# Forming the combined gate and up weight blocks on POOL instead of VectorE, in a two-layer decoder trunk

## The chip, the core and the metric

The kernel runs on one core of a Trainium2 chip. The metric is the device time of one execution in microseconds (us), the median of three runs. Five engines run side by side, each through its own queue, in order: PE (TensorE, matrix products), DVE (VectorE), ACT (ScalarE), POOL (GpSimd) and SP (SyncE, which here only issues DMAs). They wait for each other by semaphores, so an instruction that waits also holds back everything behind it in its queue.

## The reference

Two decoder layers on a stream of 1024 tokens by 1024 features. Layer 0 mixes with a convolution module, layer 1 with stick-breaking attention. Both layers end in the same feed-forward part, which is where the change lies:

```python
def conv_gated_ffn(x, w_up, w_gate, conv_w, conv_b, w_down):
    u = x @ w_up
    g = causal_dwconv(x @ w_gate, conv_w, conv_b)
    return (jax.nn.silu(g) * u) @ w_down
...
        ffn = conv_gated_ffn(x, ffn_w_up[i], ffn_w_gate[i], ffn_conv_w[i], ffn_conv_b[i], ffn_w_down[i])
        ple = jax.nn.sigmoid(x @ ple_w_gate[i]) * (p[i] @ ple_w_proj[i])
        x = layer_norm(DN_ALPHA * x + ffn + ple, ln_ffn_g[i], ln_ffn_b[i])
```

All inputs are float32; w_up and w_gate are 1024 by 2816, w_down is 2816 by 1024.

## The kernel before

Every float32 product is made of three products of rounded parts: a number is split into a high part (rounded, made by ACT) and a low part (the number less its high part). `mm3` (L136 to L139) issues high by high (L137), high by low (L138) and low by high (L139); for a weight as the stationary side, L137 and L138 need its high part and L139 its low part.

The feed-forward part (`ffn_phase`) first adds the sigmoid-gated term `ple` (L246 to L261, which uses POOL at L259 and DVE at L261), then forms sums and differences of blocks of x (L276 to L284), and then loops over the 2816 hidden columns, 256 at a time, in 11 steps (L389). In each step `gate` makes 256 columns of x @ w_gate, `down` (for the step before) multiplies 256 hidden columns with w_down and adds the result to the residual tiles (L383, DVE), and `up` makes 256 columns of x @ w_up. `gate` and `up` both call `fast`, which computes a 2 by 2 block product with seven block products instead of eight (Strassen's scheme in Winograd's form). Its left factors are blocks of the weight and sums of them, its right factors blocks of x and sums of them.

`fast_w` (L286) prepares the left factors of one `fast`. Two DMAs from SP (L290) bring the halves r0 (with blocks a11, a12) and r1 (a21, a22). Four additions, L294, each 128 partitions by 512 numbers, form s1 = a21 + a22, a21 = a11 - a21 in place, s2 = s1 - a11 and, after a12 has been split, a12 = a12 - s2 in place. Seven `split` calls make the high part on ACT (L299) and the low part on POOL (L300, shown by the profile as L86, the line of the helper `sub_l`). There are 2 layers x 11 steps x 2 = 44 calls of `fast_w`, so 176 additions at L294.

All weight tiles come from one pool `wp` of eight slots, shown as `w`: the raw halves, the sums and the split parts, and the raw, high and low tiles of w_down (`load_w`, L126 to L133). One `fast_w` takes ten such tiles, so a tile is written only when PE, POOL or ACT has finished with the one that had its slot.

The seven block products go to PSUM tiles; DVE adds them up (L322). In `gate`, ACT and DVE then apply the three convolution taps (L348, L353) and ACT the silu (L355). In `up`, DVE multiplies (L364) and splits (L367, shown as L86 `f<-f`). The PSUM tiles (`big0`, `big1` and `bank0` to `bank3`) are used in turns by two groups of four halves; `down` writes its halves in turn, and the fifth may begin only when L383 has read the first.

The order of instructions in each queue is set when the kernel is built, by a scheduler that places them by its own estimates of durations (`schedule_with_timeline_sim`); the code above gives only what depends on what.

Of the kernel before, what the change touches and what calls it, by code (L numbers as in the profile page):

```python
# [51 lines left out]
def trunk_kernel(ctx: ExitStack, tc, x, p, a_pw1_w, a_pw1_b, a_dw_w, a_dw_b, a_ln_g, a_ln_b, a_pw2_w, a_pw2_b,  # L52
                 b_wq, kv_wk, kv_wv, b_wo, ln_mix_g, ln_mix_b, ffn_w_up, ffn_w_gate, ffn_conv_w, ffn_conv_b,
                 ffn_w_down, ple_w_gate, ple_w_proj, ln_ffn_g, ln_ffn_b, out, stop=None):
    nc = tc.nc
# [29 lines left out]
    def sub_l(eng, l, full, h):  # L85
        eng.tensor_tensor(out=l, in0=full, in1=h.bitcast(F32), op=ALU.subtract)  # L86
# [11 lines left out]
    def wslot(dt=F32):  # L98
        return wp.tile([P, 1024], dt, name="w", align_bytes=A4)
# [23 lines left out]
    def w_slab(src, kts, cols):  # L123
        return src.rearrange("(k p) n -> p k n", p=P)[:, kts, cols]
# [111 lines left out]
    def ffn_phase(i, xT, res, pp, g, b, sb, finish):  # L236
# [49 lines left out]
        def fast_w(w, f):  # L286
            cs = slice(f * P, (f + 2) * P)
            r0, r1, s = (wslot().rearrange("p (k n) -> p k n", k=4) for _ in range(3))
            for kb, r in enumerate((r0, r1)):
                nc.sync.dma_start(out=r, in_=w_slab(w[i], slice(kb * 4, kb * 4 + 4), cs))  # L290
            n0, n1 = slice(0, P), slice(P, 2 * P)

            def add(out, a, c, op):
                nc.vector.tensor_tensor(out=out, in0=a, in1=c, op=op)  # L294

            def split(full):
                hl = wslot(F32R).rearrange("p (o k n) -> p o k n", o=2, k=4)
                h, l = hl[:, 0], hl[:, 1]
                nc.scalar.copy(out=h, in_=full)  # L299
                sub_l(nc.gpsimd, l, full, h)  # L300
                return h, l

            a11, a21, a12, a22, s1, s2 = (t[:, :, ns] for t in (r0, r1, s) for ns in (n0, n1))
            add(s1, a21, a22, ALU.add)
            add(a21, a11, a21, ALU.subtract)
            add(s2, s1, a11, ALU.subtract)
            ws = [split(t) for t in (a11, s2, s1, a21, a12)]
            add(a12, a12, s2, ALU.subtract)
            return ws + [split(a12), split(a22)]
# [583 lines left out]
```

## Time and profile before

| what | value |
|---|---|
| median of 3 runs | 2701.26 us (2700.6 to 2705.1) |
| the profiled execution, its own time | 2710.24 us |
| its span, first to last instruction | 2708.1 us |
| PE busy | 2530.3 us (93%) |
| DVE busy | 1797.4 us (66%) |
| POOL busy | 1219.6 us (45%) |
| ACT busy | 1045.1 us (39%) |
| feed-forward loop of layer 0 | about 532 to 1190 us of the span |
| feed-forward loop of layer 1 | about 1990 to 2680 us |

The profile is of one execution. Its own time is 0.33% above the median. "Busy" is the time in which an engine works on an instruction. Matmuls overlap on PE, so PE can be busy without a gap and still be slower than it could be; the distance from one start to the next tells its pace.

### The profile page before, as it was taken

How to read it: one execution, taken by the hardware profiler on the slowest of the kernel's cores; microseconds unless marked ns; L12 is line 12 of the kernel's file. 1: busy time of each engine (PE TensorE's matmuls, PEld its weight loads, DVE VectorE, ACT ScalarE, POOL GpSimd, SP SyncE). 2: the span in 40 equal slices, each digit the busy share in tenths (PEclk: the TensorE clock that was granted, in tenths of full speed). 3: DMA queues.
4: the chain of work that ended last, by engine and by line, in shares of the span. 5: the costliest groups of instructions: out<-in, count | busy, mean ns of one | idle time of the engine just before them, and what ended most of it. 6: DMA issues, size and time to landing. Idle time of an engine off the chain costs nothing.

```text
span 2708.1 us, 34235 instructions
## 1 busy us (share of the span) xinstructions
PE 2530.3 (93%) x13300; PEld 2151.5 (79%) x13300; DVE 1797.4 (66%) x2785; ACT 1045.1 (39%) x1621; POOL 1219.6 (45%) x825
## 2 busy tenths in 40 slices
PE   8996898999999999999999999789899999999995
PEld 6884888987878787878888887589798787787874
DVE  4999769465565655675667677777845555655558
ACT  4556532333223332314555566632333232323231
POOL 3998236534333443413443433544744343333354
PEclk9998999999999999999999999899899999999998
DMA  4114421211111111123111101322111121111121
GB/s 151 47 47 148 163 71 63 86 47 50 47 60 47 55 55 55 40 80 108 46 43 36 55 25 47 129 84 87 63 63 62 48 63 47 47 47 47 47 78 62
DMA packets 149085, 179.12 MB, mean 66 GB/s; under 512 B 6508, under 2 KB 125756, under 8 KB 148924
## 3 DMA queue, kind: packets, MB, share of 16 engines
q1 hardware_dynamic: 144316, 168.56, 19.6%
q10 hardware_dynamic: 4608, 8.39, 0.8%
q8 instruction: 104, 1.70, 0.3%
q14 instruction: 57, 0.47, 0.1%
HBM read 151.76 MB, written 20.97 MB: 64 GB/s over the span
## 4 chain that ended last, share of the span: by engine, by line
PE 68%; DVE 18%; POOL 5%; DMA 3%; issue 3%; ACT 3%; SPq 0%; POOLq 0%; ACTq 0%; DVEq 0%
PE bank L137 13%; PE bank L138 13%; PE bank L139 13%; PE big L137 8%; PE big L139 7%; PE big L138 7%; POOL w L86 3%; PE big L739 2%; POOL pb L491 2%; DVE bank L502 2%; DVE bank L509 2%; DMA w<-in_ffn_w_up 2%; DVE pt L282 2%; PE bank L773 1%; PE more L779 1%
## 5 line engine op out<-in xcount | busy, mean ns | idle before, releaser
L86 POOL TENSOR_TENSOR w<-w 128x512 fp32r<-128x512 f32 (+1 forms) x444 | 757.7, 1720 | 1081.5 <-ACT w L299 697.0
L137 PE MATMUL bank<-w,xT 128*128 128x256 f32 x1280 | 369.7, 291 | 37.7 <-ACT sg L258 23.7
L299 ACT CAST w<-w 128x512 fp32r<-128x512 f32 x308 | 180.1, 619 | 540.2 <-PE bank L139 142.1
L138 PE MATMUL bank<-w,xT 128*128 128x256 f32 x1280 | 368.8, 290 | 2.1 <-POOL w L86 2.1
L139 PE MATMUL bank<-w,xT 128*128 128x256 f32 x1280 | 367.7, 290 | 0.7 <-DVE xT L86 0.6
L137 PEld LDWEIGHTS bank<-w,xT 128*128 128x128 f32 x1280 | 250.8, 197 | 41.0 <-ACT sg L258 25.1
L760 POOL TENSOR_TENSOR res<-res,rr 128x639 f32<-128x639 f32 (+3 forms) x96 | 152.6, 1590 | 259.7 <-DVE rr L758 237.9
L758 DVE TENSOR_TENSOR_SCAN rr<-rr,ctile 128x127 f32<-128x127 f32 (+7 forms) x128 | 195.7, 1550 | 102.5 <-ACT rr L756 102.1
L138 PEld LDWEIGHTS bank<-w,xT 128*128 128x128 f32 x1280 | 251.5, 197 | 3.4 <-POOL w L86 3.0
L139 PEld LDWEIGHTS bank<-w,xT 128*128 128x128 f32 x1280 | 250.2, 196 | 1.7 <-DVE xT L86 1.3
L132 ACT CAST w<-w 128x1024 fp32r<-128x1024 f32 x136 | 142.9, 1051 | 227.5 <-PE bank L138 60.5
L137 PE MATMUL big<-xT,w 128*128 128x512 f32 x544 | 212.3, 390 | 0.4 <-DVE xT L86 0.4
L138 PE MATMUL big<-xT,w 128*128 128x512 f32 x544 | 211.9, 389 | 0.0
L139 PE MATMUL big<-xT,w 128*128 128x512 f32 x544 | 211.9, 389 | 0.0
L294 DVE TENSOR_TENSOR w<-w 128x512 f32<-128x512 f32 x176 | 130.1, 759 | 106.1 <-DMA w<-in_ffn_w_up 52.1
L137 PE MATMUL bank<-xT,w 128*128 128x512 f32 x496 | 200.0, 403 | 0.3 <-DVE m L86 0.2
L138 PE MATMUL bank<-xT,w 128*128 128x512 f32 x496 | 198.2, 400 | 0.0
L139 PE MATMUL bank<-xT,w 128*128 128x512 f32 x496 | 197.8, 399 | 0.0
L383 DVE TENSOR_TENSOR m<-m,bank 128x512 f32<-128x512 f32 x192 | 128.8, 682 | 82.2 <-PE bank L139 82.1
L137 PE MATMUL bank<-w,f 128*128 128x512 f32 x448 | 170.3, 395 | 7.8 <-ACT f L366 4.3
L138 PE MATMUL bank<-w,f 128*128 128x512 f32 x448 | 176.1, 393 | 0.0
L139 PE MATMUL bank<-w,f 128*128 128x512 f32 x448 | 173.8, 391 | 0.0
(162 smaller groups left out, 5941.3 us busy)
## 6 DMA issues: line engine op xcount, KB each, us to landing
w<-in_ffn_w_gate SPq DMA_DIRECT2D x44, 512.0 KB
w<-in_ffn_w_up SPq DMA_DIRECT2D x44, 512.0 KB
w<-in_ffn_w_down SPq DMA_DIRECT2D x44, 512.0 KB
w<-in_a_pw_w SPq DMA_DIRECT2D x32, 512.0 KB
pp<-o ACTq DMA_DIRECT2D x32, 256.0 KB
w<-in_ple_w_gate SPq DMA_DIRECT2D x16, 512.0 KB
w<-pp SPq DMA_DIRECT2D x16, 512.0 KB
w<-in_b_wo SPq DMA_DIRECT2D x16, 512.0 KB
```

The costliest lines, as they stand in the source:

```text
L86: eng.tensor_tensor(out=l, in0=full, in1=h.bitcast(F32), op=ALU.subtract)
L132: nc.scalar.copy(out=h[:, 0:n], in_=raw)
L137: nc.tensor.matmul(out=o, lhsT=sh, rhs=mh, start=first, stop=False)
L138: nc.tensor.matmul(out=o, lhsT=sh, rhs=ml, start=False, stop=False)
L139: nc.tensor.matmul(out=o, lhsT=sl, rhs=mh, start=False, stop=last)
L282: nc.vector.tensor_tensor(out=f, in0=a, in1=c, op=ALU.subtract)
L294: nc.vector.tensor_tensor(out=out, in0=a, in1=c, op=op)
L299: nc.scalar.copy(out=h, in_=full)
L383: nc.vector.tensor_tensor(out=rv, in0=rv, in1=ps, op=ALU.add)
L491: nc.gpsimd.tensor_tensor(out=pb, in0=pb, in1=pr, op=ALU.add)
L758: nc.vector.tensor_tensor_scan(out=rv[:, i, 1:n][:, ::-1], data0=rv[:, i, 1:n][:, ::-1], data1=zero.broadcast_to([P, n - 1]), initial=1.0, ...
L760: nc.gpsimd.tensor_tensor(out=av[:, :, 0:n - 1], in0=av[:, :, 0:n - 1], in1=rv[:, :, 1:n], op=ALU.mult)
```

## The change

The additions at L294 are issued to POOL instead of DVE. The operation, its operands and its place in the code are the same.

```diff
             def add(out, a, c, op):
-                nc.vector.tensor_tensor(out=out, in0=a, in1=c, op=op)
+                nc.gpsimd.tensor_tensor(out=out, in0=a, in1=c, op=op)
```

The second `add` in `fast` (L322) is another function and stays on DVE. Since the scheduler places all instructions anew, orders and slots shift on every engine.

On DVE, at the end of the second step's `gate` in layer 0 (products in bank0 to bank3) and the start of `down` (halves in big0 and big1): bank tiles are gate products, f_5651 and f_5659 the gate's two output tiles, m_2587 a residual tile, w_5791 and w_5792 the raw halves for the next `up`, w_5793 its sums. Before:

```order
L322 TENSOR_TENSOR bank0_82<-bank0_82,pt_5557 128x512
L294 TENSOR_TENSOR w_5793<-w_5791,w_5792 128x4x128
L353 SCALAR_TENSOR_TENSOR f_5659<-bank3_85,ctile_86,f_5659 128x511
L322 TENSOR_TENSOR bank1_83<-bank1_83,pt_5584 128x512
L294 TENSOR_TENSOR w_5791<-w_5791 128x4x128
L294 TENSOR_TENSOR w_5793<-w_5793,w_5791 128x4x128
L353 SCALAR_TENSOR_TENSOR f_5659<-bank3_85,ctile_86,f_5659 128x510
L353 SCALAR_TENSOR_TENSOR f_5651<-bank0_82,ctile_86,f_5651 128x512
L353 SCALAR_TENSOR_TENSOR f_5651<-bank1_83,ctile_86,f_5651 128x511
L322 TENSOR_TENSOR bank2_84<-bank2_84,pt_5584 128x512
L383 TENSOR_TENSOR m_2587<-m_2587,big0_81 128x512
```

The same place now:

```order
L322 TENSOR_TENSOR bank0_82<-bank0_82,pt_5557 128x512
L353 SCALAR_TENSOR_TENSOR f_5659<-bank3_85,ctile_86,f_5659 128x511
L322 TENSOR_TENSOR bank1_83<-bank1_83,pt_5584 128x512
L353 SCALAR_TENSOR_TENSOR f_5659<-bank3_85,ctile_86,f_5659 128x510
L353 SCALAR_TENSOR_TENSOR f_5651<-bank0_82,ctile_86,f_5651 128x512
L353 SCALAR_TENSOR_TENSOR f_5651<-bank1_83,ctile_86,f_5651 128x511
L322 TENSOR_TENSOR bank2_84<-bank2_84,pt_5584 128x512
L353 SCALAR_TENSOR_TENSOR f_5651<-bank0_82,ctile_86,f_5651 128x512
L353 SCALAR_TENSOR_TENSOR f_5651<-bank1_83,ctile_86,f_5651 128x510
L383 TENSOR_TENSOR m_2587<-m_2587,big0_81 128x512
```

The three additions that stood between the last gate work and the first L383 are gone from DVE's queue.

On POOL, from the end of one `up` (w_5411 to w_5418) through the next `gate` (raw halves w_5527 and w_5528, sums w_5529; low parts w_5535 to w_5554). Before:

```order
L86 TENSOR_TENSOR w_5411<-w_5392,w_5411 128x512
L86 TENSOR_TENSOR w_5415<-w_5392,w_5415 128x512
L86 TENSOR_TENSOR w_5418<-w_5392,w_5418 128x512
L86 TENSOR_TENSOR w_5535<-w_5527,w_5535 128x512
L86 TENSOR_TENSOR w_5538<-w_5529,w_5538 128x512
L86 TENSOR_TENSOR w_5541<-w_5529,w_5541 128x512
L86 TENSOR_TENSOR w_5544<-w_5527,w_5544 128x512
L86 TENSOR_TENSOR w_5547<-w_5528,w_5547 128x512
```

Now:

```order
L86 TENSOR_TENSOR w_5411<-w_5392,w_5411 128x512
L294 TENSOR_TENSOR w_5392<-w_5392,w_5393 128x4x128
L86 TENSOR_TENSOR w_5415<-w_5392,w_5415 128x512
L86 TENSOR_TENSOR w_5418<-w_5392,w_5418 128x512
L294 TENSOR_TENSOR w_5529<-w_5527,w_5528 128x4x128
L86 TENSOR_TENSOR w_5535<-w_5527,w_5535 128x512
L294 TENSOR_TENSOR w_5527<-w_5527 128x4x128
L294 TENSOR_TENSOR w_5529<-w_5529,w_5527 128x4x128
L86 TENSOR_TENSOR w_5538<-w_5529,w_5538 128x512
L86 TENSOR_TENSOR w_5541<-w_5529,w_5541 128x512
L86 TENSOR_TENSOR w_5544<-w_5527,w_5544 128x512
L86 TENSOR_TENSOR w_5547<-w_5528,w_5547 128x512
```

The additions stand in POOL's queue in front of the low parts that need them, and the first addition of a `gate` or `up` stands there until both raw halves have landed.

On PE, in that `gate`, at the turn from its first block product (bank0) to the second. Before:

```order
L137 MATMUL bank1_83<-tT_4773,w_5538 128x512
L138 MATMUL bank1_83<-tT_4774,w_5538 128x512
L139 MATMUL bank1_83<-tT_4773,w_5538 128x512
L137 MATMUL bank1_83<-tT_4773,w_5538 128x512
L138 MATMUL bank1_83<-tT_4774,w_5538 128x512
L139 MATMUL bank1_83<-tT_4773,w_5538 128x512
L137 MATMUL bank1_83<-tT_4773,w_5538 128x512
```

Now:

```order
L137 MATMUL bank1_83<-tT_4773,w_5538 128x512
L138 MATMUL bank1_83<-tT_4774,w_5538 128x512
L137 MATMUL bank2_84<-tT_4771,w_5541 128x512
L138 MATMUL bank2_84<-tT_4772,w_5541 128x512
L137 MATMUL bank3_85<-tT_4775,w_5544 128x512
L138 MATMUL bank3_85<-tT_4776,w_5544 128x512
L139 MATMUL bank1_83<-tT_4773,w_5538 128x512
```

PE now takes the first two matmuls of three products, which need high parts only, before the first matmul that needs a low part (L139).

## Rows read from the trace of the kernel before

**Rows 1.** The page: span and busy time of each engine.

```profile
span 2708.1 us, 34235 instructions
PE 2530.3 (93%) x13300; PEld 2151.5 (79%) x13300; DVE 1797.4 (66%) x2785; ACT 1045.1 (39%) x1621; POOL 1219.6 (45%) x825
```

**Rows 2.** Window of layer 0's loop: length, busy time (count) by engine, granted clock, DMA share, GB/s.

```profile
680.00:800.00 120.00, 116.46 (x503) 94.91 (x503) 70.55 (x99) 36.91 (x52) 46.63 (x31) 0.99 0.15 44
```

**Rows 3.** Waits of PE, whole span: waiting and awaited instruction, us, times, longest.

```profile
PE big L137 <- DVE m L383: 24.9, 16, 3.0
```

**Rows 4.** Timeline of PE at the first long wait: start, length, instruction, idle before.

```profile
651.74 0.39 PE L138 MATMUL big<-w,f 128*128 128x512 f32 x1
651.97 0.39 PE L139 MATMUL big<-w,f 128*128 128x512 f32 x1
655.21 0.69 PE L137 MATMUL big<-w,f 128*128 128x512 f32 x1 [2.86 <-DVE m L383]
...
658.97 0.39 PE L137 MATMUL bank<-xT,w 128*128 128x512 f32 x1
```

**Rows 5.** Timeline of DVE there.

```profile
644.23 0.70 DVE L322 TENSOR_TENSOR bank<-bank,pt 128x512 f32<-128x512 f32 x1 [1.12 <-PE bank L139]
647.94 1.59 DVE L294 TENSOR_TENSOR w<-w 128x512 f32<-128x512 f32 x1 [3.01 <-DMA w<-in_ffn_w_up]
...
650.71 1.28 DVE L294 TENSOR_TENSOR w<-w 128x512 f32<-128x512 f32 x2
...
654.49 0.67 DVE L383 TENSOR_TENSOR m<-m,big 128x512 f32<-128x512 f32 x1
```

**Rows 6.** Windows of 20 us: without a wait, with long waits, with a short one.

```profile
620.00:640.00 20.00, 20.00 (x90) 16.56 (x89) 12.76 (x17) 8.34 (x13) 14.06 (x10) 1.00 0.21 67
...
648.00:668.00 20.00, 17.14 (x69) 13.74 (x68) 13.15 (x19) 6.03 (x8) 4.14 (x4) 0.91 0.00 1
898.00:918.00 20.00, 18.42 (x82) 14.93 (x81) 12.21 (x19) 7.08 (x11) 5.57 (x4) 1.00 0.03 11
2360.00:2380.00 20.00, 17.14 (x76) 13.87 (x75) 13.27 (x20) 6.54 (x9) 4.99 (x5) 1.00 0.00 1
684.00:704.00 20.00, 19.61 (x87) 15.92 (x86) 10.75 (x15) 7.80 (x11) 9.87 (x7) 1.00 0.16 53
```

**Rows 7.** Groups by line and shape: busy us, mean ns, then idle before and releasers.

```profile
L294 DVE TENSOR_TENSOR w<-w 128x512 f32<-128x512 f32 x176 | 130.1, 759 | 106.1 <-DMA w<-in_ffn_w_up 52.1 <-POOL w L86 50.6 <-DMA w<-in_ffn_w_gate 2.7
L86 POOL TENSOR_TENSOR w<-w 128x512 fp32r<-128x512 f32 x308 | 405.5, 1336 | 707.5 <-ACT w L299 697.0 <-DVE big L322 8.6 <-DVE f L353 1.9
L86 POOL TENSOR_TENSOR w<-w 128x1024 fp32r<-128x1024 f32 x136 | 352.3, 2590 | 374.0 <-ACT w L132 324.0 <-PE bank L139 19.5 <-DVE norm L179 5.9
L280 POOL TENSOR_TENSOR pt<-xT 128x512 f32<-128x512 f32 x32 | 50.9, 1613 | 10.9 <-DVE xT L86 10.2 <-DVE tT L86 0.6
L86 DVE TENSOR_TENSOR f<-f 128x1024 fp32r<-128x1024 f32 x44 | 71.4, 1640 | 3.5 <-ACT f L366 3.5
```

**Rows 8.** Timelines of POOL and ACT, from the end of `up` to the next `up`.

```profile
614.31 3.79 POOL L86 TENSOR_TENSOR w<-w 128x512 fp32r<-128x512 f32 x3 [18.04 <-ACT w L299]
...
626.50 5.05 POOL L86 TENSOR_TENSOR w<-w 128x512 fp32r<-128x512 f32 x4 [3.15 <-ACT w L299]
...
636.88 6.70 POOL L86 TENSOR_TENSOR w<-w 128x1024 fp32r<-128x1024 f32 x2 [1.33 <-ACT w L132]
...
625.80 1.66 ACT L299 CAST w<-w 128x512 fp32r<-128x512 f32 x3 [5.27 <-DVE w L294]
```

**Rows 9.** Timeline of PE: the `up`'s third product, and the `gate`'s first.

```profile
616.68 0.50 PE L137 MATMUL big<-tT,w 128*128 128x512 f32 x1 [0.22 <-ACT pt L326]
...
627.71 0.39 PE L137 MATMUL bank<-xT,w 128*128 128x512 f32 x1
```

**Rows 10.** The chain that ended last, at that place: start, us, what.

```profile
643.61 4.24 DMA w<-in_ffn_w_up
```

**Rows 11.** Window in attention's last part, columns as in Rows 2.

```profile
1680.00:1740.00 60.00, 44.14 (x228) 33.30 (x226) 47.23 (x60) 38.81 (x67) 21.99 (x15) 0.89 0.24 80
```

## The prediction

> **What bounds the kernel now.** I read the page first: PE is busy for 2530.3 of 2708.1 us, DVE for 66% and POOL for 45% [rows 1]. The loop that the change touches is tighter still. In 120 us of it, about two steps, PE is busy for 116.46 us, DVE for 70.55 and POOL for 46.63 [rows 2]. So no saving of DVE time counts by itself. Only a stretch in which PE stands still can be won, and only one in which it comes to stand still can be lost.
>
> The view of PE's waits says where it stands. Over the whole span the longest entry is PE waiting for DVE's L383, the addition that frees a PSUM half for `down`: 24.9 us in 16 waits, the longest 3.0 [rows 3]. All 16 lie in the two feed-forward loops, eight per layer; in each layer four are long (2.9 us, one in each layer less or without the after-effect told below) and four short (0.4 us).
>
> The timelines of the first long wait say why L383 was late. PE has finished four halves of `down` at 651.97 and starts the fifth at 655.21, released by L383 [rows 4]. DVE had begun nothing between 644.9 and 647.94: it stood for 3.01 us at an L294, whose weight half was still on its way from memory; that transfer is also on the chain that ended last, with 4.24 us [rows 5, 10]. From there to L383, at 654.49, it did three L294, four L353 and two L322. So PE waited for an addition that nobody needed yet, because it stood at the head of DVE's queue.
>
> What one such wait costs is more than its 2.86 us. From 651.97 to 655.21 are 3.24 us where the pace is 0.23, so 3.01 are lost; the nine starts from 655.21 to 658.97 take 3.76 us where they would take 2.07, so 1.69 more are lost at a lower clock [rows 4]. The granted clock over those 20 us is 0.91 of the 2.4 GHz level; the engine had been idle just before it fell. Together 4.70 us. The windows agree: 20 us without a wait hold 90 matmuls, those with this wait 69, and 21 matmuls at 20/90 = 0.222 us are 4.7 us [rows 6]. Six of the eight long waits have this window of 69. One (898 us) was shorter and has 82, so 1.8 us; one (2360 us) kept its clock at 1.00 and has 76, so 3.1 us [rows 6]. Sum: 6 x 4.7 + 1.8 + 3.1 = 33.1 us. A short wait has 87, so 0.7 us, and eight of them 5.4 us [rows 6].
>
> **The change, part by part.** *Taken from DVE:* 176 L294, 130.1 us busy, and the 106.1 us for which DVE stood before them, 54.8 of it for transfers and 50.6 for POOL [rows 7]. DVE is no bound, so this saves only what PE waited for. I work out when the first L383 comes without them, in the frame of rows 4 to 10 and at PE's pace of 0.227. The gate's first product starts at 627.71 [rows 9], and eight products of twelve matmuls, one of them the last of `up`, end at 649.5. DVE's last L322 waits for that, two L353 follow (0.66 each), and L383 can begin at about 651.6, when the first half of `down` is also ready. The new order on PE puts a product of the next `up` between the second half and the third, and there the halves of `down` go round two big tiles, so the half that L383 frees is wanted at 649.5 + 24 x 0.227 = 654.9. L383 then has 2.6 us to spare. The code and the order of DVE's queue are the same at the other long waits, so all 33.1 us go. For the eight short ones (behind L364 and the split of `up`, not behind L294) I take no change; they bound the gain at 33.1 + 5.4 = 38.5.
>
> *Added to POOL:* 176 additions of 128x512. The trace has none of L294 there. The nearest rows are the low parts of the same tiles, 1.336 us on average, and POOL's additions at L280 beside a busy DVE, 1.613 [rows 7]; three low parts in 3.79 us give 1.26 at the least [rows 8]. So 222 to 284 us; I take 1.35, the row with the same tiles, which makes 238. POOL's share in the loop goes from 46.63 to about 68 of 120 us (four `fast_w`, 16 additions). It stays under PE.
>
> The two engines slow each other when DVE has two inputs in SBUF: two low parts of 128x1024 took 6.70 us while DVE split a hidden tile, against 2.59 on average for one [rows 7, 8]. The Trainium skill (SBUF — State Buffer, Who interferes with whom) says the same as a rule: a DVE instruction with two SBUF inputs contends with a GpSimd instruction that reads SBUF, and the one that comes second waits. By that rule an addition on POOL could wait at most for the DVE splits, 44 of 1640 ns, 72 us in all if each hit one; the sum by the rows keeps 1.35.
>
> *Weights later.* POOL now works 4 x 1.35 = 5.4 us longer per `fast_w`, in series with the low parts. Whether PE feels it is read off one passage, from the end of an `up` to the next `up`, in the new orders of the queues and with each tile's slot as the new program gives it:
> - `up`'s three low parts end at 618.1 [rows 8]; addition to 619.45; high part on ACT, 0.70 from its start to the next low part (625.80 to 626.50) [rows 8]; two low parts to 622.8.
> - The second raw half for `gate` takes the slot that the `up`'s third product leaves at 616.68 + 12 x 0.227 = 619.4 [rows 9], lands 4.24 later at 623.65 [rows 10]. Addition to 625.0, low part of a11 to 626.3, two additions to 629.0, ACT 0.70, low part of s2 to 631.0. PE wants it after 24 + 6 matmuls from 627.71, at 634.5. Spare: 3.5 us.
> - Four more low parts and the last addition to 637.6; the last two low parts end at 639.5, where the last product starts at 646.8.
> - `down`'s two low parts, at the slow 3.35 each, end at 646.2, wanted at 649.5. Spare: 3.3.
> - The next `up`: its first raw half starts to load when the first of these is done (642.9), its second when PE has finished the gate's fifth product (644.0), landing at 648.3. Addition, low part of a11 to 650.9, wanted at 652.7. Spare: 1.8. Low part of s2 at 655.6, wanted at 658.6.
>
> So nothing is late, by 1.8 us at the tightest place. Behind a POOL addition that waits for a transfer stand only low parts of the same weights, except before the first step of each layer, where some L259 stand behind three additions and a low part (5.3 us). PE writes four tiles ahead there, so I take 0; uncovered it would be 5.3 per layer.
>
> *Moved elsewhere.* The scheduler also rearranged the last part of attention. The one window of it that has room has PE busy for 44.14 of 60 us [rows 11]. I take 0, and a quarter of the idle 15.9, 4 us, to either side.
>
> **Sum.** -33.1 for the long waits, 0 for the short ones, 0 for the weights. The profiled execution would go from 2710.2 to 2677. It stands 9 us above the median of 2701.3, so the median goes to 2668. I call a difference within 0.2%, about 5 us, no change, since three runs before spread over 4.5 us.
>
> **The rivals.**
> *Part of the gain goes into a new wait.* The 1.8 us at the next `up` are used up when a transfer takes 6 us in place of 4.24, or when POOL is held by DVE's split at that moment. There are four such passages a layer. A weight 2 us late at all eight costs 16, so 2684; the case covers 2678 to 2696. For it speaks that the scheduler itself lets PE take high parts first, as if low parts came late; against it, the spare times above.
>
> *L383 stays late.* If DVE's four L353 and two L322 (654.49 - 647.94 less 2.87 of L294, so 3.7 us of work) were what held L383, nothing is won: 2701, and 2696 to 2706 with attention's uncertainty. Against it, DVE's 3.01 us of standing and 2.9 us of L294 lie in the same 10 us [rows 5], and their sum, 5.9, is more than the wait.
>
> *POOL becomes the queue that holds PE.* The place is the low part of s2 in each `gate` and the one of a11 in each `up`: about 20 passages. Up to the spare time it costs nothing. Beyond, each us costs 20 us, so it eats up the 33.1 when the low parts come 1.7 us after PE wants them. That needs them 3.5 us (a11) to 5.2 us (s2) later than I worked out, for s2 1 us more on each of five POOL instructions. At 2.5 us late it costs 50, so 2718. The Trainium skill (GPSIMD Engine Reference, 4.1 Engine selection) advises against what the change does: elementwise work belongs on VectorE, since GpSimd takes about twice as long with two inputs. The trace agrees on the ratio, 1.34 us here against 0.64 for an undisturbed L294 [rows 5, 7]. It decides only if that length lies on PE's path, which the spare times deny.
>
> **How the numbers follow.** All long waits go, 2658 to 2678: 0.60. Part: 0.17. No change: 0.10. POOL holds PE, above 2706: 0.13. The likeliest gives 2668. The range begins at 2658, where the short waits and attention also gain (33.1 + 5.4 + 4, rounded), and reaches to 2702, through the second case and over half of the third: about 0.83. Faster by over 0.2% is 0.60 + 0.17, the same 0.10, slower 0.13.
>
> **What the changed profile would show.** Right: in PE's waits the entry for L383 falls from 24.9 to about 3 us, with no wait of over 1 us and the windows of 69 matmuls near 90; L294 on POOL at 1.3 to 1.6 us; POOL near 68 of 120 us in the loop. The step on DVE is wrong if L383 still releases PE after 2 us or more. The step on weights is wrong if PE waits at L139 for POOL's low parts, or at L137 for ACT's high parts. The prediction fails most simply if the transfers for `up` and `gate` land later than 4.24 us after their slot is free, since POOL now stands for them with every low part behind it.

## The result and the profile after

The changed kernel takes 2669.02 us, median of 4 runs (2666.01 to 2669.68), beside 2701.47 us for the kernel before (2700.6 to 2705.1, 4 runs): a ratio of 0.9867, 95% interval 0.9849 to 0.9884. The forecast was 2668.0, faster. In a later repeat the change measured 2666.57 and the kernel before 2695.9, ratio 0.9898 [0.9883, 0.9913].

The page of the changed kernel, its span and the busy time of each engine, which answers to [rows 1]:

```profile
span 2667.9 us, 34126 instructions
PE 2515.0 (94%) x13300; PEld 2144.1 (80%) x13300; DVE 1665.9 (62%) x2609; ACT 1040.3 (39%) x1621; POOL 1435.4 (54%) x1001
```

DVE lost 131.5 us and 176 instructions; POOL gained 215.8 us and the same 176. Two windows of layer 0's loop, the long one that answers to [rows 2] and 20 us around the first long wait of before, which answers to [rows 6]; columns as there:

```profile
680.00:800.00 120.00, 119.33 (x526) 98.28 (x526) 59.96 (x88) 36.19 (x52) 67.06 (x48) 1.00 0.17 53
646.00:666.00 20.00, 20.00 (x90) 16.54 (x90) 11.32 (x18) 7.44 (x11) 11.12 (x9) 1.00 0.09 26
```

In the same 120 us PE now starts 526 matmuls for 503, and the 20 us that held 69 hold 90, at a granted clock of 1.00. The waits of PE over the whole span, of which four entries matter here ([rows 3] is the one of before):

```profile
PE big L137 <- ACT pt L326: 6.3, 10, 0.7
...
PE bank L137 <- DVE m L383: 3.2, 3, 1.6
...
PE bank L139 <- POOL w L86: 1.3, 1, 1.3
PE bank L138 <- POOL w L86: 1.3, 3, 0.6
```

The entry of 24.9 us in 16 waits for L383 is gone, the short ones too; the 3.2 us left are three waits after the last loop, which the kernel before has as well. Something came in: ten waits for ACT's copy L326, 2.2 us in all before, are now 6.3. One wait in the loops is for a low part from POOL, 1.3 us.

DVE and PE of the changed kernel at the place of [rows 4, 5]: first DVE, then the starts on PE that matter.

```profile
649.95 0.69 DVE L322 TENSOR_TENSOR bank<-bank,pt 128x512 f32<-128x512 f32 x1
650.54 1.40 DVE L353 SCALAR_TENSOR_TENSOR f<-bank,ctile,f 128x512 f32<-128x512 f32 x2
651.86 0.68 DVE L383 TENSOR_TENSOR m<-m,big 128x512 f32<-128x512 f32 x1
```

```profile
649.44 0.39 PE L137 MATMUL big<-w,f 128*128 128x512 f32 x1
...
652.16 0.39 PE L137 MATMUL bank<-xT,w 128*128 128x512 f32 x1
...
654.88 0.39 PE L137 MATMUL big<-w,f 128*128 128x512 f32 x1
```

L383 starts at 651.86 and is done by 652.5. PE does two halves of `down`, a product of the next `up`, and comes back to `down` at 654.88: 2.3 us to spare.

Two things moved here at once. L383 starts 2.42 us after the first matmul of `down` (649.44), where it started 5.02 us after it before (649.47 to 654.49). And PE wants the half later by one product: before, that product of `up` came behind the half that waited,

```profile
657.84 0.63 PE L137 MATMUL bank<-xT,w 128*128 128x512 f32 x1
```

and now it comes ahead of it, at 652.16. How much either does by itself is taken up with the second and the third experiment.

What the additions cost on POOL, in the groups by line and shape that answer to [rows 7], and POOL's timeline through the tight passage, which answers to [rows 8]:

```profile
L294 POOL TENSOR_TENSOR w<-w 128x512 f32<-128x512 f32 x176 | 228.2, 1308 | 115.2 <-DMA w<-in_ffn_w_up 58.7 <-DMA w<-in_ffn_w_gate 49.6 <-issue 1.7
L86 POOL TENSOR_TENSOR w<-w 128x512 fp32r<-128x512 f32 x308 | 406.9, 1339 | 370.3 <-ACT w L299 370.2
L86 DVE TENSOR_TENSOR f<-f 128x1024 fp32r<-128x1024 f32 x44 | 61.4, 1402 | 18.9 <-ACT f L366 18.9
```

```profile
623.56 1.29 POOL L294 TENSOR_TENSOR w<-w 128x512 f32<-128x512 f32 x1 [0.92 <-DMA w<-in_ffn_w_gate]
...
629.33 5.06 POOL L86 TENSOR_TENSOR w<-w 128x512 fp32r<-128x512 f32 x4 [0.73 <-ACT w L299]
...
637.35 7.59 POOL L86 TENSOR_TENSOR w<-w 128x512 fp32r<-128x512 f32 x4 [0.73 <-ACT w L299]
648.64 1.30 POOL L294 TENSOR_TENSOR w<-w 128x512 f32<-128x512 f32 x1 [3.71 <-DMA w<-in_ffn_w_up]
649.89 1.30 POOL L86 TENSOR_TENSOR w<-w 128x512 fp32r<-128x512 f32 x1
```

The standing went with the additions: POOL now sits idle for 3.71 us at the head of its queue, where DVE sat for 3.01. But behind it stand only low parts of the weights that are on their way.

Where the time came from, by a marker: L348, which runs from the first `gate` of a layer's loop to the last. Layer 0 of the kernel before, then of the changed one (shortest, median and longest in ns, first and last start in us):

```profile
L348 ACT ACTIVATE f<-big,ctile x24: 760/774/780, 549.7 to 1099.1; 128x512 f32<-128x512 f32 x24
L348 ACT ACTIVATE f<-bank,ctile x20: 769/779/783, 645.0 to 1151.5; 128x512 f32<-128x512 f32 x20
```

```profile
L348 ACT ACTIVATE f<-big,ctile x24: 758/772/782, 550.4 to 1081.5; 128x512 f32<-128x512 f32 x24
L348 ACT ACTIVATE f<-bank,ctile x20: 762/778/782, 644.9 to 1135.1; 128x512 f32<-128x512 f32 x20
```

From 549.7 to 1151.5 are 601.8 us, from 550.4 to 1135.1 are 584.7: 17.1 less. Layer 1, by the same rows, goes from 603.3 to 587.4: 15.9 less. So 33.0 us of the 40.2 by which the two profiled spans differ lie in the loops. Another 7.7 lie between the last L348 of a layer and its last L383 (68.4 to 64.6 and 82.9 to 79.0); all the rest together is under 1 us.

A correction to the texts ahead: they speak of four halves of `down` before the long wait and of the fifth as the one that waits. A half takes six matmuls here (two hidden blocks by three), so the twelve from 649.5 to 651.97 are two halves, and the third waits. It writes the second 512 columns of a tile of 1024 of which L383 reads the first 512. The times in the prediction are those of the rows and do not change; what it means is the subject of the fourth experiment.

### The profile page after: what moved, and what is told of

The parts are those of the page before. It is cut to its first block, busy times and chain, and to the rows that moved or that the text cites. A ratio compares the mean times of both kernels' runs of the same rounds, so it can differ in the third digit from the quotient of the medians.

```text
span 2667.9 us, 34126 instructions
## 1 busy us (share of the span) xinstructions
PE 2515.0 (94%) x13300; PEld 2144.1 (80%) x13300; DVE 1665.9 (62%) x2609; ACT 1040.3 (39%) x1621; POOL 1435.4 (54%) x1001
## 4 chain that ended last, share of the span: by engine, by line
PE 76%; DVE 15%; POOL 3%; issue 3%; ACT 2%; DMA 1%; SPq 0%; POOLq 0%; DVEq 0%; ACTq 0%
PE bank L137 15%; PE bank L138 15%; PE bank L139 15%; PE big L137 8%; PE big L138 8%; PE big L139 8%; PE big L739 2%; DVE bank L502 2%; DVE bank L509 2%; DVE pt L282 2%; POOL pb L491 1%; PE bank L773 1%; PE more L779 1%; PE more L778 1%; DVE tT L86 1%
## 5 line engine op out<-in xcount | busy, mean ns | idle before, releaser
L86 POOL TENSOR_TENSOR w<-w 128x512 fp32r<-128x512 f32 (+1 forms) x444 | 744.0, 1689 | 733.6 <-ACT w L299 370.2
L137 PE MATMUL bank<-w,xT 128*128 128x256 f32 x1280 | 370.2, 292 | 32.1 <-ACT sg L258 23.6
L139 PE MATMUL bank<-w,xT 128*128 128x256 f32 x1280 | 367.6, 290 | 1.6 <-DVE xT L86 1.5
L294 POOL TENSOR_TENSOR w<-w 128x512 f32<-128x512 f32 x176 | 228.2, 1308 | 115.2 <-DMA w<-in_ffn_w_up 58.7
L137 PEld LDWEIGHTS bank<-w,xT 128*128 128x128 f32 x1280 | 250.8, 197 | 35.5 <-ACT sg L258 25.0
L139 PEld LDWEIGHTS bank<-w,xT 128*128 128x128 f32 x1280 | 250.1, 196 | 2.3 <-DVE xT L86 2.0
L137 PE MATMUL big<-xT,w 128*128 128x512 f32 x544 | 213.6, 393 | 0.6 <-DVE xT L86 0.6
L139 PE MATMUL big<-xT,w 128*128 128x512 f32 x544 | 212.8, 391 | 0.0
L137 PE MATMUL bank<-xT,w 128*128 128x512 f32 x496 | 197.5, 398 | 0.3 <-DVE m L86 0.2
L139 PE MATMUL bank<-xT,w 128*128 128x512 f32 x496 | 195.9, 395 | 1.3 <-POOL w L86 1.3
L138 PE MATMUL bank<-xT,w 128*128 128x512 f32 x496 | 195.9, 395 | 0.0
L383 DVE TENSOR_TENSOR m<-m,bank 128x512 f32<-128x512 f32 x192 | 128.4, 685 | 85.7 <-PE bank L139 85.6
L138 PE MATMUL bank<-w,f 128*128 128x512 f32 x448 | 174.4, 389 | 0.0
L139 PE MATMUL bank<-w,f 128*128 128x512 f32 x448 | 173.2, 389 | 0.0
L137 PE MATMUL bank<-w,f 128*128 128x512 f32 x448 | 166.1, 391 | 4.6 <-DVE m L383 3.2
```

Of the source, the lines that this page charges most:

```text
L137: nc.tensor.matmul(out=o, lhsT=sh, rhs=mh, start=first, stop=False)
L138: nc.tensor.matmul(out=o, lhsT=sh, rhs=ml, start=False, stop=False)
L139: nc.tensor.matmul(out=o, lhsT=sl, rhs=mh, start=False, stop=last)
L294: nc.gpsimd.tensor_tensor(out=out, in0=a, in1=c, op=op)
L383: nc.vector.tensor_tensor(out=rv, in0=rv, in1=ps, op=ALU.add)
```

## The experiments

My theory: PE lost time only where it waited for L383, and L383 was late because the additions of the next `up`, with the wait for their transfer, stood ahead of it on DVE. The main rival: DVE as a whole is relieved (fewer instructions, less contention), or the scheduler's new order helps by itself. The kernels ran in three groups of four. The first and the third ran on the chip with the number 10, the second on number 1, and the kernel before had medians of 2697.89, 2695.74 and 2695.9 us beside them.

**Only the `up` weights on POOL.**

```diff
-                nc.gpsimd.tensor_tensor(out=out, in0=a, in1=c, op=op)
+                eng = nc.gpsimd if w is ffn_w_up else nc.vector
+                eng.tensor_tensor(out=out, in0=a, in1=c, op=op)
```

> Only the 88 additions of the up weights go to POOL; the 88 of the gate weights stay on DVE. Theory (L383 is late because the additions of the next up, and the wait for its transfer, stand ahead of it on DVE): the eight long waits go just as with all 176, so 2669 us, 2664 to 2675, and the entry for L383 in PE's waits is below 6 us in all. Rival (a general relief of DVE by fewer instructions, each addition worth the same): half of the 32 us, so 2685.

2670.79 us (2669.31 to 2678.84), ratio 0.9915 [0.9885, 0.9945]. The waits of PE:

```profile
PE big L137 <- DVE m L384: 3.1, 8, 0.4
PE bank L139 <- POOL w L86: 2.6, 5, 0.7
```

(L384 is L383 here.) The eight long waits are gone with half of the additions moved, and the eight short ones stay. That is the theory's number, and not the 2685 of a relief in proportion. L384 starts 2.42 us after the first matmul of `down` at all eight places, as in the change. The order on PE is another again (23 matmuls of `up` stand ahead of the third half), so this kernel does not separate the order from L384; and at five of the eight places PE now waits for a low part from POOL.

**Only the `gate` weights on POOL.** The same edit with `ffn_w_gate`.

> Only the 88 additions of the gate weights go to POOL; those of up stay on DVE. Theory: the long waits for L383 stay, about eight of 2.5 to 3 us, so 2698 us, 2692 to 2704. Rival (general relief of DVE): 2685. Rival (what helps is that the scheduler places everything anew): anywhere between, but then without long waits for L383.

2685.52 us (2681.71 to 2687.48), ratio 0.9954 [0.994, 0.9968]. My theory's 2698 was wrong, and the number is the rival's, so the trace has to say which mechanism it is. PE's waits for L384 fell to 8.8 us in 12, the long ones to 0.91 (one of them 1.86), and the first of each layer is gone:

```profile
PE big L137 <- DVE m L384: 8.8, 12, 1.9
PE bank L137 <- DVE f L354: 1.5, 2, 0.9
```

DVE before the second one, then PE:

```profile
768.38 0.69 DVE L323 TENSOR_TENSOR bank<-bank,pt 128x512 f32<-128x512 f32 x1
769.31 0.79 DVE L295 TENSOR_TENSOR w<-w 128x512 f32<-128x512 f32 x1 [0.24 <-DMA w<-in_ffn_w_up]
770.02 0.74 DVE L354 SCALAR_TENSOR_TENSOR f<-bank,ctile,f 128x510 f32<-128x510 f32 x1
770.68 1.28 DVE L295 TENSOR_TENSOR w<-w 128x512 f32<-128x512 f32 x2
...
773.80 0.67 DVE L384 TENSOR_TENSOR m<-m,big 128x512 f32<-128x512 f32 x1
```

```profile
774.52 0.50 PE L137 MATMUL big<-w,f 128*128 128x512 f32 x1 [0.91 <-DVE m L384]
```

In the new order one L354 and one L323 (L353 and L322 before) stand ahead of the first addition, and the transfer is only 0.24 us late for it. So this kernel separates by chance what the kernel before has together: three additions without the standing leave 0.91 of the 2.86 us of wait. The rest went with the standing of 3.01 us and with the first addition, which took 1.59 us there [rows 5] and takes 0.79 here. That the additions of `gate` have no part in the order of those of `up` was my error.

Six of the eight places keep PE's order of before, and they price L384's lateness alone. At five it starts 3.06 us after the first matmul of `down` (770.74 here) in place of 5.02, and the wait falls from 2.86 to 0.91; at the sixth it starts 4.01 us after it, and the wait is 1.86. So each us by which L384 comes earlier takes a us off the wait. By this the 2.42 us of the change would leave about 0.3 us of wait even in PE's old order (an estimate: 0.91 less the 0.64 from 3.06 to 2.42). At the first place of each layer PE's order has the product of `up` ahead of the third half, as in the change. There PE waits 0.6 and 0.9 us for L354 instead: the product of `up` writes the bank that L354 reads, and L354 stands in the same queue on DVE.

**The standing without the work.** The change, with an instruction of one element per partition on DVE where the first addition stood.

```diff
+            nc.vector.tensor_tensor(out=ctile[:, 352:353], in0=r1[:, 3, 255:256], in1=r0[:, 3, 255:256], op=ALU.add)
             add(s1, a21, a22, ALU.add)
```

> All additions on POOL as in the change, and on DVE, where the first addition stood, an instruction of one element per partition that reads both raw halves into a spare column: DVE stands for the transfer as before, but does none of the additions' work. PE's order is that of the change. By the timeline of the changed kernel DVE would be free again at 648.7, would have 5 L353 and 2 L322 to do (4.5 to 5.2 us), and L383 would be done by 654.6 where PE wants it at 654.9. Theory (standing and work add up, and the spare of 2.4 us takes the standing alone): 2669 to 2675 us, waits for L383 of 0.5 us at most. Rival (the standing alone made the wait, the work did not matter): eight waits of 2 to 3 us again, 2692 to 2702.

2670.71 us (2670.51 to 2671.71), ratio 0.9906 [0.9884, 0.9927], with no wait for L384 in the loops. The number is the theory's, but the test did less than it was to do: the scheduler put the instruction behind others, and at seven of the eight long places it stood for 0.32 us or less. At the eighth, the first of layer 1, it stood for 2.18 us. DVE there, then PE:

```profile
2091.59 0.16 DVE L304 TENSOR_TENSOR ctile<-w 128x1 f32<-128x1 f32 x1 [2.18 <-DMA w<-in_ffn_w_up]
...
2094.89 0.68 DVE L384 TENSOR_TENSOR m<-m,big 128x512 f32<-128x512 f32 x1
```

```profile
2094.47 0.47 PE L137 MATMUL bank<-xT,w 128*128 128x512 f32 x1 [1.16 <-DVE f L354]
```

L384 starts 4.46 us after the first matmul of `down` (2090.43), so the standing alone makes it late. PE does not wait for it, because the order of the change has the product of `up` first; but it waits 1.16 us for L354 before that product. The new order alone, with DVE still late, is therefore not free: here and at the two places of the kernel with `gate` alone it cost 0.6 to 1.2 us. The kernel before with nothing but PE's new order was not run.

The instruction over the whole span, by its line, with DVE's idle time before it; and its stand at another place:

```profile
L304 DVE TENSOR_TENSOR ctile<-w 128x1 f32<-128x1 f32 x44 | 13.5, 307 | 45.6 <-DMA w<-in_ffn_w_up 31.3 <-DMA w<-in_ffn_w_gate 13.9 <-issue 0.3
```

```profile
710.49 0.16 DVE L304 TENSOR_TENSOR ctile<-w 128x1 f32<-128x1 f32 x1 [3.09 <-DMA w<-in_ffn_w_up]
```

DVE stood for 45.6 us in all, up to 3.4 at a time, mostly at places where PE needed nothing from it, and the time did not move. Whether the standing alone would bring the wait for L384 back at all eight places stays untried.

**Take away the wait, leave the additions on DVE.** The kernel before, with four PSUM tiles of 512 columns in the feed-forward part in place of two of 1024. The core of the edit, which also splits the transposes that use these tiles (L149):

```diff
-        (b0, b2), (b1, b3) = ((t[:, 0:HALF], t[:, HALF:]) for t in (big(), big()))
+        (b0, b2), (b1, b3) = big(), big()
...
+            h = [pp_big.tile([P, HALF], F32, name=f"half{j}") for j in range(4)]
+            big = turns(((h[0], h[2]), (h[1], h[3])))
             ffn_phase(0,
```

> The kernel before, additions on DVE, but in the feed-forward part the two PSUM tiles of 1024 columns are four tiles of 512: a half of down then waits for the L383 of its own tile, that is the fifth half for the first, not the third. Theory (only the wait of PE for a late L383 costs): the fifth half is wanted 2.7 us later than the third, L383 still comes at about 654.5, so a wait of 0.2 to 0.8 us is left of 2.9: 2668 to 2680 us with all 176 additions still on DVE and about 106 us of idle before them. Rival (it is DVE's load or its contention that costs, the wait is only where it shows): 2695 to 2702.

2652.97 us (2651.89 to 2654.4), ratio 0.9839 [0.9818, 0.986]. Its page and the window of the long wait:

```profile
span 2651.4 us, 34250 instructions
PE 2508.7 (95%) x13300; PEld 2146.1 (81%) x13300; DVE 1806.6 (68%) x2785; ACT 1043.9 (39%) x1621; POOL 1198.5 (45%) x825
```

```profile
648.00:668.00 20.00, 20.00 (x90) 16.56 (x89) 15.06 (x22) 5.41 (x7) 3.77 (x3) 1.00 0.00 1
```

And DVE and PE there (L136 is L137 of before):

```profile
650.90 1.28 DVE L294 TENSOR_TENSOR w<-w 128x512 f32<-128x512 f32 x2
...
654.02 1.27 DVE L383 TENSOR_TENSOR m<-m,half 128x512 f32<-128x512 f32 x2
```

```profile
649.66 0.39 PE L136 MATMUL half<-w,f 128*128 128x512 f32 x1
...
652.38 0.39 PE L136 MATMUL half<-w,f 128*128 128x512 f32 x1
```

DVE is busier than in any other kernel here, all 176 additions are on it, L383 starts at 654.02, hardly earlier than the 654.49 of [rows 5], and PE does not wait: 90 matmuls in 20 us. With a tile for each half the third half has nothing to wait for: it starts at 652.38, before L383 has begun to read the first. The fifth is wanted 24 matmuls after the first, at 655.10, when the first L383 has been done for about 0.4 us. That the 176 additions cost time by loading DVE is refuted by this kernel; the wait was the cost, and it came from two halves sharing a tile. By the marker L348 the loops take 1164.9 us in place of 1205.1.

**Both, and all three again on one chip.** Four tiles with the additions on POOL; then the change, the four tiles, and both.

> Both: additions on POOL, and four PSUM tiles of 512 columns in the feed-forward part. Theory (both changes take away the same waits of PE for L383): nothing is added, so the time of the four tiles alone, 2653 us, 2648 to 2660, with no wait for L383 in the loops. Rival (moving the additions helps by itself, whatever L383 does): the 32 us come on top, 2621. Rival (with the wait gone, POOL's longer chain is only a cost): above 2660, with waits of PE for POOL's low parts.

> The change itself once more, on the same chip as the two kernels with four tiles, so that they can be compared. Theory: 2669 us, 2665 to 2673.

> Four PSUM tiles, additions on DVE. Theory: 2653 us, 2650 to 2657, and 12 to 20 us below the change on the same chip; rival (the distance of 16 us came from another chip): within 5 us of the change.

> Four PSUM tiles, additions on POOL. Theory: like the four tiles alone, within 4 us of them; the move of the additions is then worth nothing.

Both together took 2655.02 us (2652.32 to 2656.27) in the second group. In the third the change took 2666.57 (2665.59 to 2667.68), ratio 0.9898 [0.9883, 0.9913]; the four tiles 2654.25 (2652.96 to 2655.09), 0.9851 [0.9834, 0.9867]; both 2654.17 (2653.54 to 2658.44), 0.9855 [0.984, 0.9871]. So the four tiles beat the change by 12.3 us, and with them the move of the additions is worth nothing. In the profiles of the change and of the four tiles the loops differ by 7.2 us by the marker L348 (1172.1 and 1164.9), about what the change's ten waits for L326 (6.3) come to, which the four tiles do not have (L326 too reads one half of a tile while PE waits to write the other); the remainder lies ahead of the loops and in attention and was not taken apart.

**POOL's spare.** The change, with the first addition done twice on POOL, and then with all four done twice, each time into a spare tile first.

```diff
+                nc.gpsimd.tensor_tensor(out=spare, in0=a, in1=c, op=op)
                 nc.gpsimd.tensor_tensor(out=out, in0=a, in1=c, op=op)
```

> As the change, but the first addition of each set of weights is done twice on POOL (the first time into a spare tile): 44 more instructions of 1.3 us, all low parts behind it 1.3 us later. Theory (the tightest spare is 1.8 us): free, 2669 to 2674 us. Rival (POOL's chain is already at its limit, the prediction's third rival): up to 1.3 us in each of 44 places, 57 us, so 2690 to 2725.

> As the change, but each of the four additions is done twice on POOL: 176 more instructions, 5.2 us more for each set of weights. By the prediction's spares the low part of s2 comes 3.9 us later (spare 3.0 to 3.5), the last low parts and those of down 5.2 us later (spare 3.3): 0.4 to 0.9 us and 1.9 us late in about 20 places each, at up to 1.6 times their length: 2700 to 2760 us, with PE waiting for POOL's low parts at L139 or L138. Rival (POOL is far from the path; queues and the order on PE take it up): 2669 to 2680.

The first took 2668.73 us (2664.83 to 2670.56): 1.3 us more in each of 44 chains is free, as the spare of 1.8 us said. The second took 2693.13 (2690.03 to 2696.26), ratio 0.9989 [0.9975, 1.0004] to the kernel before: the gain is eaten, though less was lost than the 31 to 91 us that I expected. Its waits and its window of 120 us:

```profile
PE big L139 <- POOL w L86: 7.5, 8, 1.6
PE big L137 <- ACT pt L329: 7.4, 6, 1.9
```

```profile
680.00:800.00 120.00, 119.25 (x523) 97.49 (x522) 62.17 (x87) 35.53 (x51) 89.18 (x64) 1.00 0.16 53
```

Eight waits for POOL in that entry, in place of forty: in the steady loop, with POOL busy for 89 of 120 us, PE still starts 523 matmuls. The order on PE is another again there (more stretches with high parts only ahead of a low part), and my sum by fixed places left that out. The profiled span is 23.5 us longer than that of the change: 11.1 in the loops by the marker, 7.2 behind the last `gate` of the two layers, 4.4 ahead of the first one of layer 0; this was not taken apart further. So the third rival exists; it begins between a quarter more additions on POOL, which is free, and twice the additions.

**Work on DVE without a transfer.** The change, with eight, then three statistics of the finished gate tile behind the last L322, into a spare column.

```diff
             add(pc, pc, u7)
+            if w is ffn_w_gate:
+                for _ in range(8):
+                    nc.vector.bn_stats(out=ctile[:, 352:358], in_=pc)
```

> As the change, but DVE gets work of the length of the additions back, without any transfer: behind the last L322 of each gate, eight statistics of the same PSUM tile into a spare column (0.69 us each, 176 in all, 121 us). Theory (L383 waits for whatever stands ahead of it on DVE, work as well as standing, beyond a spare of 2.4 us): 5.5 us of work bring back waits of PE for L386 (the line of L383 here) of 0.5 to 3 us at the eight places, 2675 to 2700. Rival (only the standing for the transfer made L383 late): no waits, 2667 to 2673.

> As the run with eight statistics behind each gate, but with three: 66 more instructions on DVE, 46 us, again without any transfer. Theory (up to a spare of about 2.4 us before L383, work on DVE is free): 2.1 us of work at each place cost nothing, 2667 to 2673 us. Rival (DVE's busy time costs in proportion, as 14.6 us for 122): 5.5 us, so 2675.

Eight took 2683.59 us (2679.07 to 2688.32), in the range that I gave, but not by my mechanism: no wait for L386 came back in the loops. The scheduler put the statistics behind the first L386 of `down`:

```profile
656.61 0.68 DVE L386 TENSOR_TENSOR m<-m,big 128x512 f32<-128x512 f32 x1
657.20 0.69 DVE L343 BATCH_NORM_STATS2 ctile<-bank 128x6 f32<-128x512 f32 x1
```

L386 starts 2.42 us after the first matmul of `down` at all eight places, as in the change, so the theory was not tried. What grew is another wait:

```profile
PE big L137 <- ACT pt L326: 16.2, 12, 2.4
```

That is 10 us more than in the change; why L326 comes later was not taken apart. Three took 2668.97 (2667.24 to 2669.39), 2.4 us above the change on the same chip, between the free and the 5.5 us of the rival; it decides nothing. Together they say that more work on DVE is not free without limit: 122 us of statistics and the new order that came with them cost about 15. Whether work alone ahead of L383 makes PE wait for it is not shown by these two; the kernel with `gate` alone, where three additions with hardly any standing leave a wait of 0.91 us, speaks for it.

## Why the prediction was right

*All eight long waits go, 33.1 us.* Right. The waits are gone, the 20-us window has its 90 matmuls, and the loops are shorter by 33.0 (the short waits, L326 and one wait for POOL are in that, see below). L383 was worked out to start at 651.6 and started at 651.86; the half that it frees was to be wanted at 654.9 and was at 654.88. The prediction names PE's new order but does not price it apart: it is 2.72 us of that time, and without it about 0.3 us of each wait would have stayed (the estimate of the second experiment).

*What it costs to wait is more than the wait.* Right in the sum, and the kernel with `gate` alone bounds it: its waits of 0.91 us cost five or six matmuls in 20 us (85 or 84 for 90, 1.1 to 1.3 us) at a clock of 1.00.

*The short waits stay, 0 us.* Right as a sum, not in its parts: all eight went (0.39 us each, 3.1 by the waits' entries, priced at 5.4), and the waits for L326 grew by 4.1. That the two nearly cancel is luck.

*POOL takes 1.35 us for an addition, 238 us; its share 68 of 120.* Measured 1.308, 228.2 and 67.06. The slowing by DVE's splits that [rows 8] showed did not get worse: the splits on DVE even fell from 1.640 [rows 7] to 1.402 us on average.

*Nothing is late, by 1.8 us at the tightest place.* Right. The passage ran as worked out: the low part of s2 in `gate` done at 630.6 (631.0 in the sum; it is the first of the four from 629.33), `down`'s low parts at 644.9 (646.2), the next `up`'s first addition at 648.64 (648.3), its first low part done at 651.19 (650.9) where PE wanted it at 652.6. One place in the loops came late, at 2094 us, with a wait of 1.26 us; in the repeat of the change it was 0.51. That is the first rival, at one place of the eight that it was priced for. One step of the passage is miscounted: behind the low part of s2 in `gate` three low parts and not four come before the last addition, and with three the two behind it do end at 639.5.

*The prologue and attention, 0.* Within 1 us in the two profiled spans. Not in the sum were the 3.8 us per layer after the last `gate`. PE's waits there for L366, the high part of the last hidden tile, fell from 4.3 us in 2 to 1.2 in 2; the other 4.6 were not taken apart.

*The number, 2668.* It is closer to 2669.02 than the working bears out. The profiled executions differ by 40.6 us and the medians by 32.4, since the execution profiled before stood 8.8 us above its median and the one after 0.7. The sum took all 33.1 us from the slower execution, and left out the 7.7 us behind the last `gate` of the two layers. That the forecast of the median still came within about 1 us is in part luck; in the repeat the medians differ by 29.3 us.

*The reason.* That PE waited for an addition that nobody needed yet is only half of it. The kernel with four tiles shows that PE need not have waited at all: the half that stood still was free, and waited because it shares a tile with the one that L383 reads. Moving the additions made L383 early, and the order that the scheduler then set let PE ask for the half later; splitting the tile made the lateness harmless, and is worth more.

## What to carry to other kernels

Look for the instruction at the head of a queue that waits for a transfer, and ask who needs what stands behind it; moving that instruction to an engine where only its own consumers stand behind it paid here at about twice its length (1.31 us for 0.69). Then read the order on the waiting engine too: part of what a move seems to win can come from the order that was set anew with it. Before moving anything, ask whether the waiting side needs the wait: in this program a tile that holds two independent halves makes each wait for the other's readers, and a tile for each half gave more than the move and made the move worthless. And a count of places times a delay overstates a cost where the order is set anew for each kernel, as the doubled additions and the kernel with `gate` alone showed.

## What the hardware showed

An idle PE does not always come back at a lower clock. With `gate` alone on POOL, after waits of 0.91 and 1.86 us, the granted clock of the 20-us window was 1.00, as in the kernel before after the shorter of its long waits (898 us). Of that kernel's other seven, of 2.9 us, six gave 0.91 and one 1.00 [rows 6]. With the long waits gone the loop windows shown here stay at 1.00.

An addition on DVE that starts beside a low part of POOL does not end before it. An addition alone on DVE in the kernel before; then POOL there, at the place of [rows 5]; then POOL in the kernel with `gate` alone:

```profile
618.13 0.69 DVE L294 TENSOR_TENSOR w<-w 128x512 f32<-128x512 f32 x1 [0.79 <-POOL w L86]
```

```profile
647.70 1.29 POOL L86 TENSOR_TENSOR w<-w 128x512 fp32r<-128x512 f32 x1 [4.11 <-ACT w L299]
```

```profile
768.26 1.29 POOL L86 TENSOR_TENSOR w<-w 128x512 fp32r<-128x512 f32 x1 [1.87 <-ACT w L300]
```

In the first, 1.05 us of the low part lie beside the addition that started at 647.94, which took 1.59 us, 0.90 more than alone. In the second, 0.24 us lie beside the one that started at 769.31, which took 0.79, 0.10 more. Both end about 0.55 us after the low part (649.53 and 648.99; 770.10 and 769.55), and so do all 16 additions of the kernel before that start beside an instruction of POOL. So the addition waited for the low part to end. (The 0.64 us that the prediction takes for an undisturbed addition is half of a pair that overlaps; one alone takes 0.69.) The Trainium skill (SBUF — State Buffer, Who interferes with whom) has this as its rule, that of two such instructions the one that comes second waits, and here the trace agrees. It made a part of the long wait in the kernel before that the prediction did not name: the release of DVE by the transfer fell together with a low part of the same weights.
